# An attention layer split in two stages: q, k and v by seven block products in pairs of channel tiles, through DRAM, then the attention with its output projection

## The chip, the cores and the metric

The kernel runs on one core of a Trainium2 chip. The metric is the device time of one execution in microseconds (us), the median of several. The core has a matmul engine (TensorE, PE in the profile, its weight loads PEld), a vector engine (VectorE, DVE), a scalar engine (ScalarE, ACT), GpSimd (POOL), a sync engine that issues DMAs (SyncE, SP) and 16 DMA engines. TensorE writes into eight PSUM banks of 128 x 512 fp32 values.

## What is computed

The model has two layers on x of 1024 tokens by 1024 channels, all in fp32. Layer 0 mixes tokens by a gated and a convolved branch, layer 1 by attention; each is followed by a feed-forward block (FFN) with a short convolution. Only layer 1's attention is touched:

```python
h = rms_norm(x, odd_norm_g[j])
qkv = (h @ odd_w_qkv[j]).reshape(bn, s, 3, ATTN_HEADS, HEAD_DIM)
q = rotary(qkv[:, :, 0], pos)
k = rotary(qkv[:, :, 1], pos)
v = qkv[:, :, 2]
o = dilated_attention(q, k, v).astype(x.dtype).reshape(bn, s, D_MODEL)
x = x + o @ odd_w_o[j]
```

There are 16 heads of 64 channels. `dilated_attention` is the sum of three dilated patterns; the kernel computes it as one causal softmax over all keys with an additive mask that holds the logarithm of how many patterns see a key. The large products `h @ w_qkv`, `h @ w_up`, `act @ w_down` and `o @ w_o` take most of TensorE's time.

## The kernel before, in words

**Precision.** Every fp32 operand of a product is split into a high part, rounded on ACT (`hi_of`, L196), and the remainder, computed on DVE (`lo_of`, shown at L128). `mm3` (L256) then issues three matmuls for each 128 x 128 by 128 x 512 block: high x high, high x low, low x high.

**Order.** There is one program for all engines, written in order of ticks. `after(n, f)` puts work n ticks later, `tick()` moves on, and `tick` stands in the product loops about every six matmuls. So each engine has a fixed instruction order, and the DMAs have SP's. A product loop is a generator whose pieces are called units here.

**FFN up (`ffn_up`, L933).** Two pairs of channel tiles are computed plainly (`plain`), each with 96 matmuls. All further pairs are computed as a 2 x 2 block product with seven products in place of eight (`Pair`, L1094), each of 4 x 3 matmuls, 84 for a pair. The weights' sums are made on POOL (`plan`, L1020), the activations' sums once on DVE (`t_sums`), snapshots of running sums are copied by ACT (L1103).

**Attention (`attention`, L1301).** `prepare(hp)` (L1370) projects k, q and v of one pair of heads: 24 units, each of 6 matmuls into `psu` (`up_units`, L407). `rotate` (L1329) applies the rotary embedding on DVE (swap by four DMAs, two multiplications with `cos` and `sin`, one sum), then splits. `stack` copies halves of these into `k` and `st` tiles by DMAs within SBUF. `fin_v` turns v by eight transposes. All 24 units of the next pair of heads are spread over the 20 attention steps of this one by `feed`, 1.2 units a step. The loop over `steps` runs 8 head pairs x 2 heads x 10 steps. `scores` issues the score matmuls (L1430, L1431) `LEAD` = 4 steps early, `top` adds the mask and takes the maximum on DVE, `ex` takes the exponential on ACT (L1447). A step's `turn` (L1482) transposes probabilities into `ppt` and ACT and DVE split them into `tt`; `value` (L1505), two steps later, multiplies by v into `po`. ACT copies one half of `po` and DVE adds the other. `finish_pair` (L1532) scales by the inverse sums, turned and spread through DRAM, and stores `o`. The output projection runs in three groups of head pairs (`O_GROUPS`): the first within the last steps, the others behind them. `late` starts FFN 1's weights, and `then` starts FFN 1's norm for each finished token tile.

## Time and profile before

| | |
|---|---|
| median of 3 runs | 2233.28 us (2233.07 to 2234.79) |
| the profiled execution's own time | 2233.69 us |
| its span, first to last instruction | 2232.0 us |
| PE, DVE, ACT, POOL busy | 98%, 72%, 49%, 32% of the span |
| TensorE's granted clock | 0.994 of full speed |
| the attention, from its first projection to FFN 1's first product | 592.5 us |

Rows of a timeline say when an instruction started, how long it took and, in brackets, how long its engine sat idle before it and who released it. A window's row gives, for each engine, busy time and instructions within that stretch. Matmuls overlap: a single one shows some 0.39 us, but the next starts some 0.23 us after it, so time on TensorE is counted here from start to start. The attention's stretch has two parts: some 50 us of projections alone and then the steps, with projections laid between them.

### The profile page before, as it was taken

The numbers are of one execution on the slowest core, as the hardware profiler recorded it, in microseconds if no ns is written. First come the engines' busy times: TensorE is split into PE (matmuls) and PEld (weight loads), VectorE is DVE, ScalarE is ACT, GpSimd is POOL, SyncE is SP. The second block draws the span as 40 slices with busy tenths as digits, with TensorE's granted clock in tenths as the row PEclk, the third lists the DMA queues.
The fourth block names the chain that finished last, engine by engine and source line by source line (L and its number), as shares of the span: only waits on it lengthen the run. The fifth ranks groups of instructions, "written<-read, shape, count | busy, mean of one in ns | idle before, by whom it ended". The sixth has DMA issues, their size and how long they took to land.

```text
span 2232.0 us, 29238 instructions
## 1 busy us (share of the span) xinstructions
PE 2182.1 (98%) x10448; PEld 1823.9 (82%) x10448; DVE 1613.6 (72%) x2576; ACT 1098.1 (49%) x1667; POOL 705.8 (32%) x540
## 2 busy tenths in 40 slices
PE   6999899999999999999999999999999999999998
PEld 6888778888888888877888888788788888888886
DVE  6998668777777764565777777786787777777556
ACT  5345265444444545253555555654554444444532
POOL 1122033766666330040000000102456666653001
PEclk9999999999999999999999999999999999999999
DMA  5478422353534497446344444732134435349933
GB/s 185 108 140 182 148 95 73 126 184 132 193 128 175 174 363 278 142 170 152 89 107 118 123 106 123 202 110 97 66 132 154 172 136 185 132 151 346 368 133 115
DMA packets 138834, 352.13 MB, mean 158 GB/s; under 512 B 16448, under 2 KB 16832, under 8 KB 138688
## 3 DMA queue, kind: packets, MB, share of 16 engines
q1 hardware_dynamic: 133072, 329.90, 44.0%
q0 software_dynamic: 5616, 20.36, 4.6%
q8 instruction: 82, 1.34, 0.2%
q14 instruction: 64, 0.52, 0.1%
HBM read 216.01 MB, written 100.64 MB: 142 GB/s over the span
## 4 chain that ended last, share of the span: by engine, by line
PE 49%; DVE 2%; issue 2%; ACT 1%; DMA 1%; POOL 0%; DVEq 0%; POOLq 0%; ACTq 0%; SPq 0%
PE psd L1245 9%; PE psu L259 4%; PE psu L260 4%; PE psu L258 4%; PE po L1517 3%; PE psb L1069 3%; PE psb L1066 3%; PE psb L1067 3%; PE psc L1066 2%; PE psc L1069 2%; PE psc L1067 2%; PE ppt L1498 2%; PE pss L1430 2%; PE pss L1431 2%; PE ppt L1497 1%
## 5 line engine op out<-in xcount | busy, mean ns | idle before, releaser
L1245 PE MATMUL psd<-ab 128*128 128x512 f32 x1800 | 410.1, 389 | 0.0
L1245 PEld LDWEIGHTS psd<-ab 128*128 128x128 f32 x1800 | 337.7, 188 | 69.8
L258 PE MATMUL psu<-hTh,w 128*128 128x512 f32 (+1 forms) x592 | 237.0, 400 | 2.0 <-ACT hTh L196 2.0
L259 PE MATMUL psu<-hTl,w 128*128 128x512 f32 (+1 forms) x592 | 229.6, 388 | 0.2 <-DVE hTl L128 0.2
L260 PE MATMUL psu<-hTh,w 128*128 128x512 f32 (+1 forms) x592 | 229.5, 388 | 0.0
L196 ACT CAST ab<-ab 128x1024 fp32r<-128x1024 f32 x150 | 156.0, 1052 | 139.4 <-PE psd L1245 57.5
L128 DVE TENSOR_TENSOR ab<-ab,ab 128x1024 fp32r<-128x1024 f32 x150 | 189.8, 1320 | 33.3 <-ACT ab L196 32.8
L128 DVE TENSOR_TENSOR x<-psd,x 128x512 f32<-128x512 f32 x152 | 102.1, 687 | 140.3 <-PE psd L1245 112.6
L128 POOL MEMSET tt<- 128x256 f32 x64 | 20.0, 313 | 462.1 <-PE po L1517 261.7
L1103 ACT COPY sn<-psb 128x512 f32<-128x512 f32 x120 | 70.4, 587 | 170.7 <-PE psb L1069 128.0
L128 POOL TENSOR_TENSOR y<-y,y 128x512 f32<-128x512 f32 x66 | 95.1, 1441 | 182.2 <-DMA act<-y 115.7
L128 DVE TENSOR_TENSOR tt<-ppt,tt 128x512 fp32r<-128x512 f32 (+1 forms) x160 | 101.3, 634 | 46.5 <-ACT tt L196 45.4
L196 ACT CAST tt<-ppt 128x512 fp32r<-128x512 f32 (+1 forms) x160 | 86.7, 542 | 97.9 <-PE ppt L1498 88.2
L260 PEld LDWEIGHTS psu<-hTh,w 128*128 128x128 f32 x592 | 112.2, 189 | 23.3
L258 PEld LDWEIGHTS psu<-hTh,w 128*128 128x128 f32 x592 | 112.5, 190 | 19.1 <-ACT hTh L196 2.2
L259 PEld LDWEIGHTS psu<-hTl,w 128*128 128x128 f32 x592 | 112.7, 190 | 17.6 <-DVE hTl L128 0.5
L128 POOL TENSOR_TENSOR s<-wr 128x512 f32<-128x512 f32 x40 | 82.5, 2064 | 119.5 <-DVE psa L128 100.7
L128 DVE TENSOR_TENSOR wl<-wr,wh 128x1024 fp32r<-128x1024 f32 x88 | 119.7, 1361 | 0.0
L128 POOL TENSOR_TENSOR sm<-sm,mhalf 128x1 f32<-128x1 f32 (+2 forms) x38 | 31.3, 825 | 274.3 <-DVE sm L128 274.3
L1447 ACT ACTIVATE p<-p,sma 128x896 f32<-128x896 f32 (+7 forms) x128 | 99.5, 778 | 37.2 <-DVE sma L128 36.6
L1517 PE MATMUL po<-tt,v 128*128 128x256 f32 x640 | 108.3, 291 | 5.0 <-DVE tt L128 3.4
L128 DVE TENSOR_TENSOR pse<-psc,sn 128x512 f32<-128x512 f32 x40 | 28.0, 699 | 115.7 <-ACT sn L1103 115.7
(253 smaller groups left out, 5869.0 us busy)
## 6 DMA issues: line engine op xcount, KB each, us to landing
wr<-in_w_up_dram SPq DMA_DIRECT2D x88, 512.0 KB, 4.4
ab<-act SPq DMA_DIRECT2D x154, 256.0 KB, 5.4
act<-y SPq DMA_DIRECT2D x66, 512.0 KB, 2.9
wq<-in_w_down_dram SPq DMA_DIRECT2D x44, 512.0 KB, 5.3
wt<-wq SPq DMA_DIRECT2D x44, 512.0 KB, 4.5
ab<-wt SPq DMA_DIRECT2D x88, 256.0 KB, 5.4
ab<-in_w_down_dram SPq DMA_DIRECT2D x66, 256.0 KB, 5.6
wr<-in_w_qkv_dram SPq DMA_DIRECT2D x24, 512.0 KB, 3.9
```

What stands on the lines that cost most here:

```text
L128: return fn(*args, **kw)
L196: nc.scalar.copy(hi, src)
L258: nc.tensor.matmul(out_ap, st[0], mv[0], start=first, stop=False)
L259: nc.tensor.matmul(out_ap, st[0], mv[1], start=False, stop=False)
L260: nc.tensor.matmul(out_ap, st[1], mv[0], start=False, stop=last)
L1066: nc.tensor.matmul(ps, st[0], mv[0], start=f, stop=False, skip_group_check=True)
L1067: nc.tensor.matmul(ps, st[0], mv[1], start=False, stop=False, skip_group_check=True)
L1069: nc.tensor.matmul(ps, st[1], mv[0], start=False, stop=e, skip_group_check=True)
L1103: nc.scalar.copy(self.sn[key], self.b)
L1245: nc.tensor.matmul(ps, a[:, c], b[:, HALF:D], start=first and k == 0, stop=last and k == 2, skip_group_check=True)
L1447: nc.scalar.activation(p, p, AF.Exp, bias=sm[:, 2:3], scale=0.125, accum_out=lsum[hp][:, c:c + 1])
L1517: nc.tensor.matmul(po[:, c], v2[:, kb, :], tt[:, z, 256 * n:256 * n + 256], start=(g == 0 and n == 0 and z == 0), stop=(g == j and n == 1 ...
```

## The change

The attention becomes a class with two stages. `ffn_up`'s machinery is pulled out as `up_phase`, and FFN and attention both use it.

**First stage (`project`).** q, k and v are computed as 11 pairs of channel tiles by `up_phase`: v of heads 0 to 7 in two plain pairs, then nine pairs by seven block products (eight of a k and a q tile, one of two v tiles). A tile is copied out by ACT; k and q are rotated as before, v is turned as before, and the high and low parts are stored to DRAM (`store`): 48 DMAs of 512 KB in all, 32 of them for k and q. The norm ahead of it now also copies the transposed tiles (`raw`) and stores four of them (`keep`).

**Second stage (`run`).** The twelfth pair (v of heads 12 to 15) is computed plainly as the first filler (`late_units`), after its block of activations is fetched again. `load_set` fetches k, q and v of a head pair from DRAM in seven DMAs: six of 512 KB, each into 64 partitions, for k and q, and one of 1 MB for v; that of the next pair is issued ten ticks into a pair's 20 steps. Score matmuls keep their number and size but multiply the stacked high and low parts of k by q's high part and then by q's low part. The scaled minimum replaces the maximum and its scaling by a small DVE instruction. `LEAD` is 7, `VLAG` 4. The zero blocks of `tt` are set once, in four tiles. ACT copies both halves of `po`; their sum and the scaling by the inverse sums move from DVE to POOL (but for the last head pair). Scores of a head start at the steps that `S_STEPS` lists.

**Fillers.** `units` has 16 units of the late pair, 16 of the output projection for head pairs 0 and 1, and 32 for 2 to 4; `feed` asks for 0.25 to 0.4 units a step, and a filler that isn't ready gives its place up. Head pairs 5 to 7 are projected at the end, six banks opened ahead of the last head pair's part. x goes through DRAM between these groups.

**Queues.** The loads of mask, cos and sin move from POOL's queue to SP's, the store of the inverse sums from SP's to ACT's.

```diff
-O_GROUPS = ((0, 1, 2), (3, 4), (5, 6, 7))
+O_GROUPS = ((0, 1), (2, 3, 4), (5, 6, 7))
...
+QKV_ORDER = (("v", 0), ("v", 1), ("kq", 0), ("kq", 1), ("kq", 2), ("kq", 3),
+             ("kq", 4), ("kq", 5), ("kq", 6), ("kq", 7), ("v", 2), ("v", 3))
...
+LEAD = 7
+VLAG = 4
+SET_AT = 11
+O_PACE = 5
+O_LAST_AT = 12
+O_OPEN = 6
+S_STEPS = ((3, 0, 0), (3, 1, 1), (2, 0, 4), (2, 1, 5), (0, 0, 7), (0, 1, 8), (1, 0, 8), (1, 1, 9))
+LATE_SPLIT = 6
+LATE_FIRST = 6
+O_RATES = (0.25, 0.25, 0.3, 0.3, 0.3, 0.4, 0.4, 0.4)
...
+        def __init__(self, raw=False, keep=None):
...
+                if hT.keep is not None and i >= 4:
+                    nc.sync.dma_start(hT.keep[i - 4], src[0])
...
+    def up_phase(n_pairs, src, consumer, each=lambda j: None):
...
+            def src(j):
+                kind, n = QKV_ORDER[j]
+                ms = (KT + n, n) if kind == "kq" else (2 * KT + 2 * n, 2 * KT + 2 * n + 1)
+                return [io["w_qkv"][m].rearrange("p k c -> p (k c)") for m in ms]
...
+            def each(j):
+                if j == N_PLAIN:
+                    self.cos, self.sin = (stile(name=k) for k in ("cos", "sin"))
+                    nc.sync.dma_start(self.cos, io["cos"])
+                    nc.sync.dma_start(self.sin, io["sin"])
+                if j == len(QKV_ORDER) - 2:
+                    self.mask = stile(name="mask")
+                    nc.sync.dma_start(self.mask, io["mask"])
+                    after(SET_AT, lambda: self.load_set(0))
+                    after(2, self.late_weights)
+            self.start, self.products = up_phase(len(QKV_ORDER) - 1, src, self.heads, each)
...
+        def late_block(self):
+
+            raw = htile([P, 4, HALF], F32, "hr")
+            nc.sync.dma_start(raw, self.hT.keep.rearrange("i p c -> p i c"))
...
+        def late_units(self):
+            j = len(QKV_ORDER) - 1
+            outs, cv = {}, self.heads(j)
+            for t in range(2):
+                while t and not self.late_ready:
+                    yield "wait"
+                yield from up_units(self.hT, self.late_w, outs,
+                                    lambda n, t: cv.put(n, t, outs[(n, t)]), halves=(t,))
...
+            class Take:
+                def put(self, n, t, c):
+                    if not seen[n]:
+                        raw[n] = stile(name="r" + kind)
+                    nc.scalar.copy(raw[n][:, t * HALF:(t + 1) * HALF], c)
...
+                        if kind == "kq":
+                            att.rotate(raw[n], (att.q if n else att.k)[m])
+                        else:
+                            att.turn_v(raw[n], 2 * m + n)
+            return Take()
...
+            def store():
+                for z in range(2):
+                    nc.sync.dma_start(dst[z], f32v(st["hl"[z]]))
...
+        def load_set(self, hp):
...
+            def load(t, z, src):
+                nc.sync.dma_start(f32v(t[z * HD:(z + 1) * HD, :, :]),
+                                  src.rearrange("(e p) s -> p e s", e=2))
+
+            def first():
+                st["q1"], st["k"] = htile([P, 2, S], name="q"), htile([P, 2, S], name="k")
+                for z in range(2):
+                    load(st["q1"], z, self.q[hp, 0])
+                for z in range(2):
+                    load(st["k"], z, self.k[hp, z])
+
+            def second():
+                q2, v = htile([P, 2, S], name="q"), htile([P, 2, S], name="v")
+                for z in range(2):
+                    load(q2, z, self.q[hp, 1])
+                nc.sync.dma_start(f32v(v), self.v[hp].rearrange("e p s -> p e s"))
+                self.sets[hp] = (st["k"], (st["q1"], q2),
+                                 v.rearrange("p e (t c) -> p e t c", c=P))
+            first()
+            after(2, second)
...
+                    for z in range(2):
+                        nc.tensor.matmul(ps[:, :ws], qs[z], k[:, a:a + ws],
+                                         start=z == 0, stop=z == 1)
...
+                after(1, top, 1)
+                after(5, ex, 2)
...
+            def diag_tiles():
+                for _ in range(VLAG):
+                    tt = stile([P, 2, HALF], F32R, name="ttd")
+                    pool.memset(f32v(tt[:, :, 0:P]), 0.0)
...
+                after(1, lambda: hi_of(tt[:, 0, c:], pt[:, c:]))
+                after(3, lambda: lo_of(tt[:, 1, c:], pt[:, c:], tt[:, 0, c:]))
...
+                        outs_o[hp] = [stile(name="o") for _ in range(2)]
...
+                        for z in range(2):
+                            o = outs_o[hp][z][e * HD:(e + 1) * HD,
+                                              half * HALF:(half + 1) * HALF]
+                            nc.scalar.copy(o, po[z * HD:(z + 1) * HD, :])
...
-                    vec.tensor_tensor(o, po[HD:P, :], o, op=ALU.add)
...
+                eng = vec if hp == KT - 1 else pool
...
+                    eng.tensor_tensor(o, o, o2, op=ALU.add)
...
+                    nc.scalar.dma_start(l_dram[hp], st["row"])
...
+                def f():
+                    eng.tensor_tensor(o, o, st["r"], op=ALU.mult)
+                    if hp < KT - 1:
+                        nc.sync.dma_start(o_dram[hp], o)
+                        if hp == O_GROUPS[0][-1]:
+                            after(4, lambda: group(O_GROUPS[0]))
...
+                after(9, d)
+                after(15, f)
...
+            def group(ks):
+                for m, (k, w) in enumerate((k, w) for k in ks for w in (True, False)):
+                    after(1 + O_PACE * m, lambda k=k, w=w: fetch(k, w))
...
+            def units():
+                yield from self.late_units()
+                for n, ks in enumerate(O_GROUPS[:-1]):
+                    while ks[0] not in xgs or not ready(ks):
+                        yield "wait"
...
+                        if i + 2 < NT:
+                            x_load(xs, i + 2)
+                        yield from down_units([o_acts[k] for k in ks], [w_o[k] for k in ks],
+                                              xs, store, tiles=[i])
+                    if n < len(O_GROUPS) - 2:
+                        after(1, lambda n=n: group(O_GROUPS[n + 1]))
...
+                    elif got == "wait":
+                        state["want"] = state["done"]
+                        break
...
+            diag_tiles()
+            while self.tails:
+                self.tails.popleft()()
+            self.late_block()
+            for _ in range(LATE_FIRST):
+                feed(1)
+                tick()
+            for gi in range(-LEAD, 0):
+                for a in s_at.get(gi, ()):
+                    do_scores(*a)
+                feed(1)
+                tick(2)
+            for gi, step in enumerate(steps):
+                hp = step[0]
+                if gi == len(steps) - O_LAST_AT:
+                    group(O_GROUPS[-1][:-1])
+                if gi % 20 == 0:
+                    after(2 * VLAG + 2, lambda hp=hp: self.load_set(hp + 1))
+                for a in s_at.get(gi, ()):
+                    do_scores(*a)
+                feed(O_RATES[hp] / 2)
+                tick()
+                turn(*step)
+                feed(O_RATES[hp] / 2)
+                if gi >= VLAG:
+                    value(*steps[gi - VLAG])
+                tick()
...
+
+            for b in banks[:O_OPEN]:
+                part(b, range(n))
+            tk.until(lambda: ready(ks))
+            late()
+            f = then(xn)
...
+        hT = Normed(True, dpool.tile([4, P, HALF], F32, tag="keep", name="keep")
+                    if ph == "attn" else None)
 
...
+        up["attn"] = Attention()
+        up["attn"].start()
...
-    attention(x_drams["attn"], hT, nxt.then, lambda: ffn_start(1))
+    att, hT = up["attn"], nxt.hT
+    att.project(hT)
+    nxt = Next("ffn1")
+    att.run(x_drams["attn"], nxt.then, lambda: ffn_start(1))
```

## Rows read from the trace of the kernel before

**Rows 1.** The page, busy time of TensorE, its share of the span and instructions

```profile
PE 2182.1 (98%) x10448; PEld 1823.9 (82%) x10448; DVE 1613.6 (72%) x2576; ACT 1098.1 (49%) x1667; POOL 705.8 (32%) x540
```

**Rows 2.** The page, the chain that ended last, by engine

```profile
PE 49%; DVE 2%; issue 2%; ACT 1%; DMA 1%; POOL 0%; DVEq 0%; POOLq 0%; ACTq 0%; SPq 0%
```

**Rows 3.** Windows: stretch, length, engines' busy time, clock, DMA share, GB/s; attention

```profile
986.40:1578.90 592.50, 583.91 (x3273) 501.89 (x3274) 430.33 (x949) 324.47 (x640) 58.67 (x88) 0.99 0.45 124
```

**Rows 4.** Windows, one head pair's steps with the next pair's projections

```profile
1246.15:1306.50 60.35, 60.35 (x355) 52.42 (x354) 46.17 (x106) 35.14 (x72) 2.81 (x9) 1.00 0.44 114
```

**Rows 5.** Timeline of TensorE: start, length, operation; two runs of six projection matmuls

```profile
1242.96 0.39 PE L258 MATMUL psu<-hTh,w 128*128 128x512 f32 x1
...
1244.33 0.27 PE L1497 MATMUL ppt<-ident,p 128*128 128x128 f32 x1
...
1252.77 0.40 PE L258 MATMUL psu<-hTh,w 128*128 128x512 f32 x1
...
1254.17 0.27 PE L1497 MATMUL ppt<-ident,p 128*128 128x128 f32 x1
1254.28 0.27 PE L1498 MATMUL ppt<-ident,p 128*128 128x128 f32 x1
```

**Rows 6.** Waits of TensorE in the attention's stretch: total, times, longest

```profile
PE po L1517 <- DVE tt L128: 3.4, 2, 3.3
PE pss L1430 <- DMA st<-rl: 2.2, 1, 2.2
PE psu L258 <- ACT hTh L196: 2.0, 1, 2.0
```

**Rows 7.** Timeline of VectorE and of GpSimd around the longest wait

```profile
1438.44 1.22 DVE L128 TENSOR_TENSOR rl<-rq,rh 128x1024 fp32r<-128x1024 f32 x1
1439.57 3.38 DVE L128 TENSOR_TENSOR w<-wr,w 128x1024 fp32r<-128x1024 f32 x1
...
1439.41 8.12 POOL L128 TENSOR_TENSOR o<-ot,o 128x1024 fp32r<-128x1024 f32 x3 [8.16 <-ACT o L196]
```

**Rows 8.** Windows, six us just behind that wait

```profile
1443.00:1449.00 6.00, 5.53 (x26) 4.82 (x27) 4.29 (x12) 3.61 (x7) 4.77 (x3) 0.72 0.97 303
```

**Rows 9.** Windows, the two FFNs' first two pairs, plain, until the block products

```profile
341.50:387.80 46.30, 46.30 (x218) 38.53 (x218) 44.38 (x66) 23.52 (x38) 15.08 (x11) 1.00 0.18 57
1578.90:1630.60 51.70, 48.29 (x218) 39.71 (x217) 43.65 (x67) 27.93 (x44) 15.85 (x11) 0.97 0.17 62
```

**Rows 10.** TensorE's timeline, second product of two neighbouring block pairs, FFN 0

```profile
500.08 0.39 PE L1066 MATMUL psa<-hTh,wh 128*128 128x512 f32 x1
...
519.12 0.39 PE L1066 MATMUL psa<-hTh,wh 128*128 128x512 f32 x1
```

**Rows 11.** Windows, that block pair's 19.04 us

```profile
500.08:519.12 19.04, 19.04 (x85) 15.77 (x84) 14.89 (x22) 9.16 (x12) 12.50 (x8) 1.00 0.21 70
```

**Rows 12.** Groups of that pair on VectorE: busy, mean ns, idle before

```profile
L128 DVE TENSOR_TENSOR y<-y,y 128x1024 f32<-128x1024 f32 x2 | 2.4, 1220 | 0.0
...
L128 DVE SCALAR_TENSOR_TENSOR y<-psb,fcw,y 128x510 f32<-128x510 f32 x1 | 0.8, 750 | 0.0
```

**Rows 13.** Windows by tile, one head pair (PE, PEld, DVE, ACT): p, tt

```profile
1246.15:1306.50 60.35, 11.11 (x72) 8.86 (x72) 13.75 (x24) 13.81 (x32) 1.00 0.44 114
1246.15:1306.50 60.35, 13.42 (x81) 11.66 (x81) 12.70 (x20) 10.83 (x20) 2.81 (x9) 1.00 0.44 114
```

**Rows 14.** Timeline of ScalarE, back to back

```profile
1255.45 0.56 ACT L196 CAST tt<-ppt 128x512 fp32r<-128x512 f32 x1
1255.92 0.58 ACT L1529 COPY o<-po 64x512 f32<-64x512 f32 x1
```

**Rows 15.** Windows with DMAs dense: eight 64-partition stack copies, then FFN down

```profile
1231.50:1241.50 10.00, 10.00 (x62) 8.81 (x61) 6.68 (x18) 5.23 (x12) 0.32 (x1) 1.00 0.98 222
800.00:840.00 40.00, 40.00 (x178) 33.12 (x177) 30.07 (x25) 18.55 (x18) 15.93 (x8) 1.00 1.02 377
```

**Rows 16.** DMA issues of one kind: KB each, median us to landing

```profile
wr<-in_w_qkv_dram SPq DMA_DIRECT2D x24, 512.0 KB, 3.9
```

696 lines of the change are left out of this document (339 added, 357 removed).

## The prediction, on record before the change was run

> **What bounds the kernel now.** I read the page first: TensorE is busy 98% of the span [rows 1], and the chain of work that ended last lies on it for 49% with nothing else above 2% [rows 2]. So the next question is what TensorE does where the change is, and that is a matter of windows. From the attention's first projection to FFN 1's first product it takes 592.5 us, 583.9 of them busy [rows 3]; in the steady part it has no gap at all: one head pair takes 60.35 us and TensorE is busy for 60.35 [rows 4], while VectorE has 46.17 and ScalarE 35.14. The projections laid between the steps are a filler. Two runs of six of them take 1.37 and 1.40 us from start to start, so 0.231 us each, and a transpose takes 0.11 [rows 5]. All waits of TensorE in the stretch are eight, 10.5 us; the three longest are shown [rows 6]. The reader should see that the saving must come from TensorE's own work, and that what is lost can come only from engines that today have slack.
>
> The stretch as a sum: 1152 projection matmuls at 0.231 are 266.1. A head pair without its filler is 60.35 - 144 x 0.231 - 9 transposes x 0.11 = 26.1, eight are 208.8. The output projection is 384 matmuls at 0.227 (a block pair's pace, 19.04 / 84 [rows 10]), 87.2. 72 turns of v and of the sums are 7.9, 64 transposes of FFN 1's norm 7.0. Together 577.0; with 10.5 of waits, 5.0 are left, about what half clock costs: an idle of 3.3 us [rows 6] is followed by a granted clock of 0.72 over 6 us [rows 8], 1.7 us lost, and there are three such places.
>
> **The change part by part.** *The new ledger without waits.* The first two pairs with the rest of the norm are the same program as FFN's first two, which took 46.3 and 51.7 us, copies and sums of the activations included [rows 9]; I take 48, nearer the first, since four token tiles of this norm are ready early, as there. Nine block pairs at 19.04 us [rows 10] are 171.4. The late pair is 96 x 0.231 = 22.2. Eight head pairs 208.8, output projection 87.2, turns 7.9, and 40 x 0.11 = 4.4 for the norm transposes that fall ahead of FFN 1. Sum 549.9: 42.6 less than now. That is the room in which all new waits must fit.
>
> *VectorE and GpSimd in the block pairs.* FFN's pair keeps VectorE busy 14.89 us [rows 11]. Its convolution goes (eight taps at 0.75, four corners of some 0.2, one product at 1.22 [rows 12]: 8.1), two rotations come (eight operations of a row's 1.22: 9.8), so 16.6 of 19.04. What speaks against a fit is that VectorE's operation took 3.38 us instead of 1.22 beside a sum on GpSimd [rows 7]. Were each of the four half-size GpSimd sums of a pair to hold VectorE for its own length (8.12 / 3 / 2 = 1.35), a pair would need 22.0 and eight pairs lose 24. FFN's pair has these four sums too and TensorE doesn't wait in it [rows 10, 11], so I take 2 of 0 to 24. The Trainium skill, page "SBUF — State Buffer", section "SBUF: two separate sides", says that a VectorE operation with two SBUF inputs and a GpSimd operation exclude each other for a whole instruction; the long row agrees, and by that rule the loss would be the 24.
>
> *Handover between the stages.* The last block pair's tails and six late units lie between the issue of the first set and the first scores, about 17 us. The old handover waited 2.2 us for a DMA [rows 6]. I take 2 of 0 to 6.
>
> *Steps without filler.* 64 units are spread by hand: 13 run ahead of the steps, three in the first 12 steps. The first output group needs head pair 1 finished, stored, fetched and split: issued ticks put it at about step 69; it lasts to step 117, and the next group is ready at about 140. So some 80 of 160 steps have attention alone, at 26.1 / 20 = 1.305 us on TensorE. There ScalarE needs, per head pair, 13.81 for p, 10.83 for tt [rows 13] and eight copies of `po` at 0.58 [rows 14], 29.3, or 1.46 a step; but back to back an operation starts 0.09 before its predecessor ends [rows 14], 44 times, so 25.3 or 1.27. VectorE has 13.75 + 12.70 [rows 13], 1.32, or some 1.25 with the same overlap; its 64-row sums and small scalings are gone. The loss is 0 to 80 x 0.16 = 12.8; I take 3, as the overlap is what the row shows and the leads (7 steps for scores, 4 for values) absorb bursts.
>
> *The sets.* Seven times the next head pair's set is issued in step 5 and its first score stands in step 13. The six DMAs needed are 3.15 MB. Eight steps give 10.4 us without filler, 13.8 or 14.9 with 0.3 or 0.4 units of 1.39 us; with the fillers where I put them the seven covers are 12.9, 10.4, 10.4, 12.1, 13.8, 14.9 and 10.4. The rows give two speeds: 377 GB/s with whole tiles in FFN down, 222 with 64-partition copies while the DMAs were as busy [rows 15]. A load of 512 KB lands 3.9 us after issue [rows 16], 2.5 more than at 377 GB/s. So a set takes 10.9 or 16.7 us: TensorE waits 1.4 or 32.0 in sum. I take 300 GB/s, midway, as the source is DRAM and not another 64 partitions: 13.0 us, waits of 9.
>
> *Half clock.* Each idle of two us or more costs 1.7 [rows 8]: three of them, 5; none to six otherwise.
>
> *Tail and the rest.* Ahead of the last head pair's part lie 20 dense units and six opened banks, some 29 us, over its finish of 15 ticks; x's trips through DRAM have two tiles of lead. If that cover fails, one load's 3.9 us a group. I take 2 of 0 to 6, and 2 for short waits as now.
>
> *At no price*, being off TensorE's path: the store of the sums on ScalarE's queue (eight), mask, cos and sin behind one pair's fetches on SP's, GpSimd's memsets gone and its sums of `o` added. On SP's queue a store of `o` waits for GpSimd, and the fetches of fillers behind it have 12 ticks before they are split; were that cover gone, a filler comes a step late and its place is only moved to the dense end.
>
> Sum of the waits: 2 + 2 + 3 + 9 + 5 + 2 + 2 = 25. 42.6 - 25 = 17.6 gained. Against the profiled execution's own 2233.69 us (span 2232.0, 1.7 around; the median is 2233.28, 0.02% less) that is **2216 us**.
>
> **The rivals.** *All covers hold.* Sets at 377 GB/s, engines overlapped, no half clock: waits of 8, 2199. For it: FFN's block pairs run without a wait [rows 10, 11].
>
> *The sets come late* (the other side). At 222 GB/s the seven sets cost 32.0 and six idles 10.2 at half clock, 42 where I have 14: 2216 + 28 = 2244, slower. It decides from waits and half clock of 31 us together, which is a set of some 12.6 us plus landing, 250 GB/s. For it: the six DMAs fill 64 partitions each, as the copies did [rows 15]. Against it: those copies also read from 64 partitions. The Trainium skill, page "SBUF — State Buffer", section "Can I just issue two DMAs to hit both halves?", says that transfers to the two halves serialize and the section on the port swizzle gives 196 to 218 GB/s for 64 partitions; the row of 222 agrees, and by that rule this rival is the outcome.
>
> *ScalarE or VectorE paces the steps* without overlap: 12.8 instead of 3, 2226.
>
> *The block pairs don't save*: GpSimd's sums hold VectorE, 24 instead of 2, 2238: the change then moves work without shortening it.
>
> **How the numbers follow.** A measurement of this kernel can tell about 0.2%, 4.5 us, from no change. Chances: forecast 0.54 (its own range, 2206 to 2229, is faster in 0.48, same in 0.04, slower in 0.02), all covers 0.12 (faster), pacing 0.08 (faster 0.07, same 0.01), no saving 0.07 (0.01, 0.04, 0.02), sets late 0.19 (0.03, 0.03, 0.13). Faster 0.71, same 0.12, slower 0.17. The range leaves out the better half of the best case and the far end of the late sets: 2198 to 2245.
>
> **What would show it.** The projections' stage should show pairs of 19.04 us and last some 220 us; with 20.8 or more the fourth rival holds. In the steps without filler a head pair should take 26 to 28 us; 29 or more with ScalarE or VectorE full is the third. TensorE's waits should name `pss` behind DMAs of q and k, about 9 us in all; 30 would be the second, near zero the first. Wrong altogether would be a wait that none of these rows has, such as PSUM banks held through the longer lags.

## The result, and the profile after

| | median | ratio to the kernel before, with its 95% interval |
|---|---|---|
| kernel before | 2233.87 us | |
| changed kernel | 2243.59 us | 1.0044, 1.0031 to 1.0057 |
| forecast | 2216 us, 2198 to 2245 | |

The change makes the kernel slower by 0.44%. The time lies at the upper edge of the range, on the other side of the forecast.

On the page TensorE is now busy 97% of the span [rows 1], and the chain that ended last lies on it for 77%, with 4% on DMAs, where it was 1% [rows 2]:

```profile
PE 2166.4 (97%) x10340; PEld 1810.0 (81%) x10340; DVE 1635.1 (73%) x2483; ACT 1153.5 (51%) x1780; POOL 796.6 (36%) x535
...
PE 77%; DMA 4%; DVE 3%; ACT 3%; issue 1%; POOL 1%; SPq 0%; POOLq 0%; ACTq 0%; DVEq 0%
```

The attention, from its first projection to FFN 1's first product, takes 600.1 us where it took 592.5 [rows 3], and it starts 2.0 us later. These are the windows of its parts (columns as in rows 3): the two plain pairs, the nine block pairs, the handover to the first turned probabilities, the steps, and the end from the last product with v.

```profile
988.46:1040.50 52.04, 51.32 (x241) 42.19 (x241) 39.36 (x57) 26.22 (x52) 16.15 (x11) 0.95 0.37 130
1040.50:1214.64 174.14, 173.40 (x768) 142.56 (x767) 148.17 (x132) 86.01 (x126) 67.24 (x40) 1.00 0.67 211
1214.64:1246.82 32.18, 27.30 (x128) 22.09 (x126) 16.30 (x35) 13.45 (x28) 0.00 (x0) 0.95 0.75 250
1246.82:1524.73 277.91, 256.31 (x1770) 232.85 (x1768) 214.58 (x572) 224.72 (x500) 49.39 (x21) 0.98 0.78 215
1524.73:1588.54 63.81, 57.91 (x269) 46.50 (x268) 33.07 (x63) 25.88 (x41) 16.87 (x12) 0.99 0.63 232
```

Length less busy time of TensorE is its idle time: 0.7, 0.7, 4.9, 21.6 and 5.9 us, 33.8 together. To see all that is lost, half clock too, I count each instruction of TensorE at the pace at which its kind follows itself without a gap (0.227 us for 512 columns, 0.176 for 384, 0.120 for 256, 0.108 for a transpose) and call the sum the work of a stretch:

| part | length | work | beyond the work |
|---|---|---|---|
| two plain pairs | 52.0 | 48.8 | 3.2 |
| nine block pairs | 174.1 | 172.7 | 1.4 |
| handover | 32.2 | 24.7 | 7.5 |
| steps | 277.9 | 244.7 | 33.2 |
| end | 63.8 | 55.6 | 8.2 |
| together | 600.1 | 546.4 | 53.7 |

By the same count the kernel before has 570.9 of work and 21.6 beyond it. So the change saves its 24.5 us of work (9 x 12 matmuls at 0.227) and loses 32 in waits and half clock, 25 of them idle time (33.8 us where [rows 3] has 8.6). A block pair is what it was to be, 19.04 us and TensorE busy throughout; the head pairs without filler are as well; three of those with filler are not. The windows: a block pair, then head pairs 1 to 4 and 6 from their first turn to the next pair's (head pairs are counted from 0; pair 5, with 34.40 us, is like its work).

```profile
1096.70:1115.74 19.04, 19.04 (x86) 15.77 (x84) 17.98 (x16) 9.11 (x13) 7.93 (x4) 1.00 0.69 222
1277.40:1303.90 26.50, 26.50 (x203) 24.94 (x202) 23.59 (x68) 25.84 (x62) 4.81 (x2) 1.00 0.74 180
1303.90:1330.80 26.90, 26.78 (x203) 25.02 (x202) 23.95 (x70) 26.27 (x62) 4.79 (x2) 1.00 0.71 184
1330.80:1371.60 40.80, 33.90 (x228) 29.28 (x227) 30.20 (x80) 31.57 (x69) 9.54 (x4) 1.00 0.88 233
1371.60:1412.60 41.00, 37.17 (x240) 33.79 (x239) 28.61 (x77) 27.56 (x62) 4.74 (x2) 0.92 0.82 217
...
1447.00:1487.60 40.60, 31.80 (x212) 28.42 (x211) 29.02 (x77) 32.96 (x71) 11.92 (x5) 0.92 0.80 230
```

Pairs 3, 4 and 6 hold 24, 36 and 9 matmuls of fillers, so 26.1 plus these at 0.227 would be 31.6, 34.3 and 28.1 us: they lose 9.2, 6.7 and 12.5. The longest waits of TensorE in the steps (in all, times, longest), and the only one on a set's transfer:

```profile
PE po L1637 <- DVE sma L142: 10.6, 2, 6.7
...
PE pss L1542 <- DMA q<-q_dram: 1.5, 1, 1.5
```

Here `po` holds the products with v, `pss` the scores, `p` the probabilities, and `sma` is the small tile of minima that VectorE writes together with `p`. The wait of 6.7 us, followed back through the timelines of ScalarE, SP, GpSimd, VectorE and TensorE (start, length, engine, operation, and in brackets the idle time before it and its releaser):

```profile
1459.23 0.31 ACTq L1673 DMA_DIRECT2D l_dram<-lrow  x1
...
1466.60 1.10 SPq L1679 DMA_DIRECT2D r<-l_dram  x2
...
1474.06 2.34 POOL L142 TENSOR_TENSOR o<-o,r 128x1024 f32<-128x1024 f32 x1 [5.52 <-DMA r<-l_dram]
...
1476.43 0.69 DVE L142 CUSTOM_DVE_ANT_0 p<-pss,mask 128x512 f32<-128x512 f32 x1 [7.50 <-POOL o L142]
...
1477.19 0.58 PE L1637 MATMUL po<-tt,v 128*128 128x256 f32 x1 [6.74 <-DVE sma L142]
```

Read it from the top: the 8 KB of inverse sums are stored at 1459.2 but the load that needs them goes out only at 1466.6, in two parts, and the second lands at 1473.9; GpSimd scales; and VectorE's `p` starts as that scaling ends. `p` doesn't read `o` or `r`: what it waits for is the buffer that the scaling gives free. So VectorE stands 7.5 us with the split of `tt` behind it, and TensorE behind that. From the store's issue to the end of the scaling it takes 19.4, 17.1 and 17.2 us for pairs 2, 3 and 5 (while pairs 3, 4 and 6 run), 15.1 for pair 4 and 9 to 12 for the others, and only in the three long ones does VectorE wait, 4.3, 5.0 and 7.5 us:

```profile
DVE p L142 <- POOL o L142: 16.9, 3, 7.5
```

So the buffers cover 15.1, 12.0 and 9.7 us of this chain in pairs 3, 4 and 6. The cover differs from pair to pair.

Why the store is late stands in the list of transfers (KB each, median us to landing) of the steps; before, l_dram's landed in 2.4 us:

```profile
q<-q_dram SPq DMA_DIRECT2D x28, 512.0 KB, 12.4
...
v<-v_dram SPq DMA_DIRECT2D x7, 1024.0 KB, 17.3
...
l_dram<-lrow ACTq DMA_DIRECT2D x7, 8.0 KB, 7.3
```

A set was in flight. The set of head pair 3, and the work of its due step (SP's timeline, then TensorE's in step 5 of pair 2 and at pair 3's first score):

```profile
1297.82 1.28 SPq L1499 DMA_DIRECT2D q<-q_dram  x2
...
1311.23 0.27 PE L1617 MATMUL ppt<-ident,p 128*128 128x128 f32 x1
...
1321.57 0.63 PE L1542 MATMUL pss<-k,q 128*128 128x512 f32 x2
```

The set goes out 13.4 us ahead of the step in which the program has it, as SP waits for semaphores and not for ticks; the last part of q lands at 1315.9, 18 us after the first issue, and is needed at 1321.6. While it runs the DMA engines are full at this rate:

```profile
1305.00:1313.00 8.00, 8.00 (x62) 7.46 (x61) 7.71 (x24) 7.84 (x20) 1.36 (x1) 1.00 1.03 223
```

That is the rate of the 64-partition copies, 0.98 and 222 GB/s [rows 15].

### The profile page after: what moved, and what is told of

It is laid out like the page before. It is cut to its first block, busy times and chain, and to the rows that moved or that the text cites. A ratio compares the mean times of both kernels' runs of the same rounds, so it can differ in the third digit from the quotient of the medians.

```text
span 2241.7 us, 29095 instructions
## 1 busy us (share of the span) xinstructions
PE 2166.4 (97%) x10340; PEld 1810.0 (81%) x10340; DVE 1635.1 (73%) x2483; ACT 1153.5 (51%) x1780; POOL 796.6 (36%) x535
## 4 chain that ended last, share of the span: by engine, by line
PE 77%; DMA 4%; DVE 3%; ACT 3%; issue 1%; POOL 1%; SPq 0%; POOLq 0%; ACTq 0%; DVEq 0%
PE psd L1275 17%; PE psb L1044 8%; PE psb L1041 8%; PE psb L1042 8%; PE psc L1044 4%; PE psc L1041 4%; PE psc L1042 4%; PE po L1637 3%; PE pss L1542 2%; PE psu L273 2%; PE psu L274 2%; PE psu L272 2%; PE psa L1044 2%; PE psa L1041 2%; PE psa L1042 2%; PE psd L274 2%
## 5 line engine op out<-in xcount | busy, mean ns | idle before, releaser
L210 ACT CAST wh<-wr 128x1024 fp32r<-128x1024 f32 x112 | 117.5, 1049 | 6.6 <-DVE rl L142 4.7
L142 DVE SCALAR_TENSOR_TENSOR acc<-h,cw,acc 128x1007 f32<-128x1007 f32 (+22 forms) x77 | 96.8, 1261 | 1.5
L1542 PE MATMUL pss<-k,q 128*128 128x512 f32 (+2 forms) x384 | 89.5, 347 | 7.0 <-DVE sma L142 2.6
L272 PE MATMUL psu<-hTh,wh 128*128 128x512 f32 x224 | 91.5, 408 | 3.7 <-ACT hTh L210 3.7
L273 PE MATMUL psu<-hTl,wh 128*128 128x512 f32 x224 | 89.8, 401 | 1.8 <-DVE hTl L142 1.8
L1204 ACT ACTIVATE y<-y 128x1024 f32<-128x1024 f32 x44 | 46.7, 1062 | 84.7 <-DVE y L142 84.7
L274 PE MATMUL psu<-hTh,wl 128*128 128x512 f32 x224 | 89.3, 399 | 0.0
L142 POOL TENSOR_TENSOR wq<-wq 128x512 f32<-128x512 f32 x44 | 78.4, 1784 | 29.8 <-issue 14.6
L142 DVE CUSTOM_DVE_ANT_0 p<-pss,mask 128x512 f32<-128x512 f32 (+3 forms) x128 | 71.0, 564 | 24.2 <-POOL o L142 16.9
L142 DVE SCALAR_TENSOR_TENSOR y<-psb,fcw,y 128x511 f32<-128x511 f32 (+3 forms) x160 | 76.9, 483 | 12.2 <-ACT y L1170 6.8
## 6 DMA issues: line engine op xcount, KB each, us to landing
q<-q_dram SPq DMA_DIRECT2D x32, 512.0 KB, 11.7
```

The costliest lines, as they stand in the source:

```text
L142: return fn(*args, **kw)
L210: nc.scalar.copy(hi, src)
L272: nc.tensor.matmul(out_ap, st[0], mv[0], start=first, stop=False)
L273: nc.tensor.matmul(out_ap, st[0], mv[1], start=False, stop=False)
L274: nc.tensor.matmul(out_ap, st[1], mv[0], start=False, stop=last)
L1542: nc.tensor.matmul(ps[:, :ws], qs[z], k[:, a:a + ws], start=z == 0, stop=z == 1)
```

## Experiments: is it the sets, and by which way

Theory A: a set of 4.2 MB at 222 GB/s delays the small transfers of the head pair before, and VectorE stands for a buffer. Rival B: lags, buffers and ScalarE's pace, whatever the DMAs do. Ratios are to the kernel before, run beside each; "idle" is TensorE's in the steps, 21.6 us in the changed kernel.

**Two sets only.**

```diff
+            if hp >= 2:
+                self.sets[hp] = self.sets[hp - 2]
+                return
```

> Head pairs 2 to 7 fetch nothing and use the q, k and v of pairs 0 and 1 instead; the instructions of all engines stay as they are. Theory A (a set of 4.2 MB delays the 8 KB store and the broadcast load of the inverse sums that are issued behind it, GpSimd's scaling comes late, the buffers it holds are missing for VectorE's next probabilities, TensorE waits): the store lands in 2 to 3 us instead of 6.1, VectorE's 16.9 us of waiting for GpSimd go to under 3, TensorE's idle time in the steps falls from 21.5 us to under 8, the time by 18 to 28 us to 2216 to 2226. Theory B (the longer lags of 7 and 4 steps and the steps without filler are short of buffers and of ScalarE whatever the DMAs do): not under 2236.

2228.8 us, ratio 0.9981 (0.9971 to 0.9991). The steps as a window, and two rows of the lists:

```profile
1248.22:1509.91 261.69, 251.77 (x1770) 228.62 (x1769) 214.57 (x572) 224.13 (x500) 49.52 (x21) 1.00 0.41 132
...
l_dram<-lrow ACTq DMA_DIRECT2D x8, 8.0 KB, 1.3
...
DVE p L142 <- POOL o L142: 2.0, 1, 2.0
```

Idle 9.9, and 16.2 us less in the steps: that is the price of the sets, half of all that the steps lose beyond their work. It lies in head pairs 3, 4 and 6 alone: here they take 37.4, 34.4 and 34.5 us, 16.1 less together, and the other five are within 0.3 us of what they were. Theory A holds, 3 us below the gain that it named, and B (not under 2236) is not the whole. The 9.9 us still idle have no set behind them; that B's lags, buffers and ScalarE's pace cause them is not shown. Without six of the sets the change is 0.2% faster than the kernel before, where its 24.5 us of saved work alone would be 1.1%.

**The q and k part earlier.** `third` loads v, 22 ticks after q and k.

```diff
+SET_STEP = 14
...
+            if late:
+                after(late, third)
...
-                if gi % 20 == 0:
-                    after(2 * VLAG + 2, lambda hp=hp: self.load_set(hp + 1))
+                if gi == 0:
+                    after(2 * VLAG + 2, lambda: self.load_set(1))
+                if gi % 20 == SET_STEP:
+                    self.load_set(hp + 2, 2 * (20 - SET_STEP) + 2 * VLAG + 2)
```

> The q and k part of a set is issued 11 steps earlier, in step 14 of the pair before the last, and v's 1 MB stays where it is, so that the store and the load of the inverse sums find 1 MB ahead of them and not 4.2 MB. Theory A: VectorE's waits for GpSimd under 5 us, the waits of 3.8 and 6.7 us at the value products gone, 12 to 20 us faster than the changed kernel, 2224 to 2232. Theory A2 (it is the volume in each pair, not the order, that delays the small transfers): within 4 us of 2243.6. Theory B: within 4 us as well.

2250.1 us, 1.0072 (1.0057 to 1.0087): slower. VectorE's and ScalarE's waits in the steps:

```profile
DVE p L143 <- POOL o L143: 2.0, 1, 2.0
...
ACT o L211 <- DMA ot<-o_dram: 10.2, 1, 10.2
ACT w L211 <- DMA wr<-in_w_o_dram: 8.8, 2, 5.7
```

The first row is what A forecast, and the gain is gone all the same: now ScalarE's splits wait in order for the fillers' transfers, which share the time with the sets. So the order chooses who waits. That the volume in a pair, at this rate, is what delays (A2) fits; but A2's time, within 4 us of 2243.6, was missed as well, by 2.5 us.

**The sum and the scaling of o back on VectorE.**

```diff
-                eng = vec if hp == KT - 1 else pool
+                eng = vec
```

> The sum of the two halves of o and the scaling by the inverse sums go back from GpSimd to VectorE for all head pairs. Theory A (the load of the inverse sums is late, and what waits for it holds up those behind): VectorE itself now waits for the load with the next probabilities behind it, so the waits grow: 4 to 25 us slower than the changed kernel. Rival E (GpSimd's 2.4 us in place of 1.2 is what makes the chain late): 3 to 8 us faster.

2251.9 us, 1.0075 (1.0059 to 1.0092), 7 to 8 us slower than the changed kernel; VectorE waits for the load itself, 26.3 us where it waited 16.9 for GpSimd:

```profile
DVE o L142 <- DMA r<-l_dram: 26.3, 6, 8.0
```

So GpSimd's slower scaling isn't the cause; it shelters VectorE from part of the lateness.

**A shorter lead.**

```diff
-LEAD = 7
+LEAD = 5
```

> The scores run 5 steps ahead in place of 7, so that a set is needed two steps (2.6 us) later and two steps' probabilities less are held. Theory A (VectorE's probabilities wait for a buffer that the scaling of o frees): VectorE's waits for GpSimd fall from 16.9 us to under 10, 3 to 8 us faster, as long as the shorter lead covers mask, exponential and turn. Theory B' (the lead is what lets ScalarE and VectorE absorb their bursts): the steps without filler go from 26.5 to over 28 us a head pair, 4 to 12 us slower.

2241.3 us, 1.0033 (1.0022 to 1.0045), some 2 us faster, which isn't clear of noise and less than A's 3 to 8. VectorE's wait for GpSimd:

```profile
DVE p L142 <- POOL o L142: 4.4, 1, 4.4
```

It is 4.4 us in place of 16.9, though the chain of the inverse sums still takes 17 to 19 us in four head pairs: with two steps' probabilities less to hold, the buffers cover more of it, so the link is the buffer. Head pairs without filler take 27.1. But idle is still 20.3 us: TensorE's turns now wait for the probabilities themselves, some 12 us, so what the buffers gave, the shorter lead took.

**The first set after the last swaps.**

```diff
-SET_AT = 11
+SET_AT = 15
```

> The first set is issued four ticks later, behind the four swap transfers of the last rotation. Theory A says that ScalarE's wait of 10.2 us for that rotation and TensorE's of 3.8 us behind it came from these swaps standing behind the set: they go to under 4 and under 0.5, and the time falls by 3 to 6 us to 2238 to 2241. The rival is that the first scores then wait for the set themselves, by the 4 to 5 us that it comes later: no gain, or up to 4 us lost.

2244.2 us, 1.0049 (1.0034 to 1.0064): no gain. ScalarE's wait for the last rotation fell from 10.2 to 2.4 us and TensorE's of 3.8 behind it went, as A said; but then the block of activations of the late pair (`hr`, 1 MB) stood behind the set, ScalarE waited 9.3 us for it and TensorE, behind ScalarE and VectorE, 6.0:

```profile
ACT hTh L210 <- DMA hr<-keep: 9.3, 1, 9.3
```

## Experiments: why a set is slow

Theory C: because each q or k transfer fills 64 partitions. A packet here is a row of 4 KB; share x 16 engines x 4096 bytes / rate is the time of one: 1.03 x 16 x 4096 / 223 GB/s = 303 ns. v's transfers fill 128. The Trainium skill, page "SBUF — State Buffer", section "Door 1: The DMA port swizzle", gives some 218 GB/s as the limit for 64 partitions and twice that for 128; 223 agrees with it.

**Both halves in one transfer.**

```diff
-                nc.sync.dma_start(f32v(t[z * HD:(z + 1) * HD, :, :]),
-                                  src.rearrange("(e p) s -> p e s", e=2))
...
+                    nc.sync.dma_start(f32v(t[:, e, :]), src(e))
...
+                return lambda e: x[e * HD:(e + 1) * HD, :].unsqueeze(0).to_broadcast([2, HD, S])
```

The source of a transfer is 2 x 64 rows of 1024.

> The same 3.15 MB of k and q of each set are fetched by six transfers into all 128 partitions (one for each half of the columns) in place of six into 64. Theory C (the set is slow because each transfer fills 64 partitions: 4 KB packets take 305 to 315 ns in them and 159 ns in v's, which fills 128): the packets take about 160 ns, a q or k transfer lands some 6 us after issue in place of 11.7, the waits behind the sets (16.2 us by the kernel with two sets) mostly go, time 2228 to 2234, and the first set's wait shrinks too. Rival D (the rate is that of reading DRAM while other transfers run): packets stay near 300 ns, time within 3 us of 2243.6.

2614.5 us, 1.1703 (1.1686 to 1.1721), which neither side forecast. A window in a set:

```profile
1385.00:1405.00 20.00, 3.03 (x18) 2.10 (x16) 3.40 (x12) 4.24 (x13) 0.00 (x0) 0.67 0.13 52
```

A share of 0.13 is two of 16 engines. The Trainium skill, page "DMA: Bandwidth & Descriptors", section "Rules for kernel authors", says that an outermost dimension smaller than 16 confines a transfer to as many engines; with two it agrees. The run tells nothing of C but that 0.13 x 16 x 4096 / 52 = 164 ns a packet.

**Two queues.**

```diff
-                nc.sync.dma_start(f32v(t[z * HD:(z + 1) * HD, :, :]),
+                (nc.scalar if z else nc.sync).dma_start(f32v(t[z * HD:(z + 1) * HD, :, :]),
```

> Of each pair of transfers that fill the two halves of a tile of q or k, the second is issued on ScalarE's queue, so that both halves are written at the same time. Theory C (a transfer into 64 partitions is slow because of where it writes): with both halves in flight the packets of 305 to 315 ns come down towards 160, the set takes some 11 us in place of 17, the fourth, fifth and seventh head pairs get shorter by 10 to 15 us in all, 2229 to 2235. Rival D (the rate is the same however the halves are ordered): packets stay at some 310 ns, and ScalarE's issues, 0.6 us each, cost another 0 to 4 us: 2243 to 2248.

2258.4 us, 1.0104 (1.0089 to 1.0119), 10 us beyond the slower forecast. It doesn't tell C from D: the halves were not written at once, as ScalarE reached its issue 7.7 us after SP:

```profile
1308.04 0.60 SPq L1499 DMA_DIRECT2D q<-q_dram  x1
...
1315.77 0.60 ACTq L1499 DMA_DIRECT2D q<-q_dram  x1
```

**q and k laid out in DRAM as in the tiles.**

```diff
+                    for e in range(2):
+                        x = f32v(st["hl"[z]])[e * HD:(e + 1) * HD, :]
+                        for d in range(2) if is_q else (z,):
+                            to = dst[z, e] if is_q else dst[e]
+                            nc.sync.dma_start(to[d * HD:(d + 1) * HD, :], x)
...
+                    nc.sync.dma_start(f32v(t[:, e, :]), src[e])
```

> q and k are laid out in DRAM as they stand in the tiles, q twice, so that each of the six transfers of a set fills 128 partitions from 128 rows of 4 KB; the stores ahead are cut into pieces of 64 rows and there are 1 MB more of them per block pair. The kernel with a two-part outer dimension kept only three DMA engines busy, at 159 ns a packet, so it did not tell theories C and D apart; this one does. Theory C: packets of some 160 ns on all engines, the set lands in 11 us, the waits of the steps fall from 33.2 us beyond the work to some 18 to 22, the block pairs keep 19.04 us: 2229 to 2234. Rival D: packets near 300 ns, no gain in the steps; and if the stores load the queue of the block pairs, some us more: 2243 to 2250.

2260.8 us, 1.0115 (1.01 to 1.013): both outcomes at once, in different stages. Block pairs, steps, and two transfers in the steps:

```profile
1043.17:1248.40 205.23, 184.54 (x768) 147.90 (x766) 149.32 (x132) 84.99 (x126) 64.92 (x40) 0.95 0.75 219
1283.94:1546.38 262.44, 253.35 (x1770) 230.03 (x1769) 214.01 (x571) 223.51 (x500) 49.50 (x21) 0.99 0.63 227
...
q<-q_dram SPq DMA_DIRECT2D x28, 512.0 KB, 7.2
...
l_dram<-lrow ACTq DMA_DIRECT2D x7, 8.0 KB, 2.1
```

The steps give back 15.5 us with the full volume still fetched, so C holds there. The block pairs lose 31; their stores are now twelve to a pair, in pieces of 64 rows, and 1 MB more, and this run alone doesn't part the two.

**Heads interleaved.** The channels of two heads stand alternately, and a tile of a set is every second of 256 rows: one stride, 128 partitions, whole stores.

```diff
-                    nc.sync.dma_start(dst[z], f32v(st["hl"[z]]))
+                    for to in (dst[z, 0], dst[z, 1]) if is_q else (dst[z],):
+                        nc.sync.dma_start(to, f32v(st["hl"[z]]))
...
+                rows = src.rearrange("z (p e) s -> e (z p) s", e=2)
+                    nc.sync.dma_start(f32v(t[:, e, :]), rows[e])
...
+        "w_qkv": heads_mixed(up(i["odd_w_qkv"][0])),
```

> The channels of the two heads of a q or k tile stand alternately (the columns of the weights and the rows of cos and sin are permuted for it), so that a tile of a set is every second row of 256 rows in DRAM: each of the six transfers fills 128 partitions with one stride, k needs no other store than before, q is stored twice in whole tiles (1 MB more a block pair), and a rotation's swap takes two transfers in place of four. Theory C: packets of 160 ns in the sets, the steps lose about 16 us less as with the relaid sets, and the block pairs keep 19.04 us as their stores are whole: 2226 to 2231 us, faster than the changed kernel by 13 to 17 and than the kernel before by 2 to 8. If the block pairs lose as with the relaid sets, it was the added volume and not the pieces: 2245 to 2260.

2231.6 us, 0.9991 (0.9982 to 1.0), 12 us faster than the changed kernel and 0.6 us past the far end of what was expected; the interval just reaches 1, so it is hardly clear of the kernel before. Block pairs, steps, a window in a set, and a store:

```profile
1041.25:1221.73 180.48, 174.99 (x768) 142.11 (x767) 145.98 (x132) 84.86 (x126) 68.50 (x40) 1.00 0.73 249
1252.26:1512.93 260.67, 251.55 (x1770) 228.74 (x1769) 213.72 (x571) 223.55 (x500) 49.50 (x21) 1.00 0.66 229
...
1310.00:1312.00 2.00, 2.00 (x17) 1.86 (x16) 2.00 (x9) 1.94 (x4) 0.00 (x0) 1.00 1.03 422
...
l_dram<-lrow ACTq DMA_DIRECT2D x8, 8.0 KB, 2.4
```

422 GB/s at the same share, 160 ns a packet, and the steps are as short as with two sets (260.7 to 261.7), though all sets are fetched. C is shown: the form of the transfers, not their bytes, cost the 16 us. The block pairs lose 6.3 with the same bytes stored as in the relaid sets, so some 25 of the 31 us there came with the pieces.

**The same with q stored once**, its four transfers back at 64 partitions, only k's two at 128 (the diff is that of the last, less its second store).

> Interleaved heads, but q is stored once, as in the changed kernel, and still fetched by four transfers into 64 partitions; only k's two transfers fill 128. A set then needs some 2.1 MB at 220 GB/s and 2.1 MB at 400, 15 us in place of 17 to 19. If the six us that the interleaved heads lose in the block pairs come from q's second store, they are back: 174 us from the first to the last block product. If the waits behind the sets have a threshold at the cover that the chain of the inverse sums has, most of the 17 us stay won (steps 18 to 24 us beyond their work): 2225 to 2231. If they go with the time of the set, a fifth of them: 2238 to 2241.

2234.7 us, 1.0007 (0.9995 to 1.0018), between the two forecasts. Block pairs, steps, VectorE's wait for GpSimd:

```profile
1041.08:1215.21 174.13, 173.35 (x768) 142.56 (x766) 150.16 (x132) 85.20 (x126) 67.78 (x40) 1.00 0.65 213
1247.13:1518.30 271.17, 254.71 (x1769) 232.53 (x1768) 214.01 (x571) 223.97 (x500) 49.51 (x21) 0.97 0.77 220
...
DVE p L142 <- POOL o L142: 10.9, 2, 10.2
```

The second store is what the block pairs paid for. TensorE has one long wait in the steps in place of three, of 9.1 us in pair 6; from the store of the sums to the end of the scaling it took 19.9 us there, 15.0 and 12.8 in pairs 3 and 4, and VectorE waited 10.2, nothing and 0.7. The chain less the wait gives 9.7 us in pair 6 and 12.1 in pair 4, the covers of the changed kernel again; in pair 6 it is 9.7 with two sets only and with interleaved heads too (a chain of 11.7, a wait of 2.0). So the loss has a threshold, but not one: what counts is by how much the chain exceeds the cover of its pair. The steps lost 26.5 us beyond their work, more than the 18 to 24 of the threshold's forecast, as a single chain was long where the cover is shortest.

## Experiments: the rest

**The last weight.** Two runs, the split 5 ticks after the fetch in place of 12, and the rows fetched 12 steps earlier and split where they were fetched, with the load of the norm's gain (in `then`) ahead of FFN 1's first weights:

```diff
-                after(12, parts)
+                after(n, parts)
...
-                        after(1, lambda: fetch(KT - 1, True))
+                        after(1, lambda: fetch(KT - 1, True, 5))
---
+                    after(2 + 4 * O_PACE, last_load)
...
-                        after(1, lambda: fetch(KT - 1, True))
+                        after(1, last_split)
...
+            f = then(xn)
             late()
-            f = then(xn)
```

> The weight rows of the last head pair are split 5 ticks after their fetch instead of 12. If the late weight (its split ended at 1552.8 us, with six banks open) is why the next norm starts late and TensorE waits for it in the last 30 us, the norm starts some 5 us earlier, these waits fall from about 6 to 2 us and the time by 3 to 5 us. If the norm's own chain over ScalarE, GpSimd and VectorE sets the pace there, the time stays within 1.5 us of 2243.6.

> The last head pair's weight rows are fetched some 12 steps earlier and split where they were fetched, and the norm's gain is issued ahead of FFN 1's first weights. Theory F (in the end SP's queue stands behind the stores of x, so that the last weight was issued at 1545 us, and the next norm starts late): the weight is split by about 1536 us, x's first tile is ready some 10 us earlier, the tail from the last product with v to FFN 1's first product falls from 63.8 to about 57 us, the time by 5 to 7 us to 2236.5 to 2238.5. Rival G (the norm's own pace of 5.5 us a tile over four engines is the limit): under 2 us gained.

2243.2 us, 1.0047 (1.0031 to 1.0064), and 2240.4, 1.003 (1.0018 to 1.0042). In the second the weight was split at 1545 us in place of 1553, yet x's first tile came only 2 us earlier, as the opened banks stand ahead of it; the end shortened from 63.8 to 63.0, FFN 1's first pairs by 2.4. The 3 us gained lie between F's 5 to 7 and G's 2, and the run doesn't part the weight from the gain's load. TensorE's waits in the end for the norm's `xn` are 3.6 us with and without the change, so the norm's own chain (G) stays where it was.

**The splits apart**, alone:

```diff
-O_PACE = 5
+O_PACE = 9
-                after(3 if hp < KT - 1 else 1,
+                after(6 if hp < KT - 1 else 1,
```

> The fetches of a group of the output projection stand 9 ticks apart in place of 5, and o counts as split after 6 ticks in place of 3. In the kernel with two sets the fourth and the seventh head pair still took 5.8 and 6.4 us more than their work. Theory H (four to six splits in a burst, 1.05 us each on ScalarE and 1.2 to 2.4 on VectorE or GpSimd, fall on steps in which these engines have no slack): these two head pairs get 3 us shorter each, the time falls by 3 to 7 us. Rival: the splits only come later, and fillers with them, to the dense end: within 2 us of 2243.6.

2249.1 us, 1.0068 (1.0053 to 1.0083): slower by 5.5, for a reason that neither side named: the fetches moved into the next set, and ScalarE waited for `ot`, a tile of `o` fetched again:

```profile
ACT o L210 <- DMA ot<-o_dram: 8.6, 2, 8.4
```

**Combinations:** relaid sets with the last weight; interleaved heads with the last weight; these with the splits 8 ticks apart; the same with q stored once; and with the second store 11 ticks later.

> The relaid sets together with the early last weight. The two losses lie in different stages, so the gains add: with theory C 2225 to 2232, 2 to 4 us under the relaid sets alone, which would be level with the kernel before or up to 8 us under it.

> Interleaved heads together with the early last weight, which alone gained 3 us: 2223 to 2229, some 3 us under the interleaved heads alone.

> As the last, with the fetches of a group 8 ticks apart in place of 5 and o counted as split after 6 ticks in place of 3. With slow sets this cost 5.5 us, as ScalarE stood waiting for o's transfers. Theory H (bursts of splits cost the fourth and the seventh head pair 5.8 and 6.4 us, and with fast sets nothing hides it any more): 3 to 6 us faster than with 5 ticks. Rival (fillers come later and are missing in the steps): 0 to 5 us slower.

> As the last, with the early last weight and the fetches of a group 8 ticks apart. With a threshold: 2222 to 2228, faster than both kernels. Without: ScalarE waits for o's transfers again as with the splits apart alone, 2240 to 2248.

> As the interleaved heads with the early last weight and the splits apart (2229.6), but q's second store is issued 11 ticks later, behind the next block pair's swaps, which it delayed (a swap landed 3.7 us after issue in place of 2.3, with VectorE, ScalarE and TensorE behind it). If this delay is what the block pairs lost (180.5 to 181.8 us in place of 174.1), most of the 6 to 7 us come back: 2222 to 2226. If it is the buffers that q's parts hold until their second store, they are held longer now: 2230 to 2240.

| run | median | ratio | interval |
|---|---|---|---|
| relaid, last weight | 2258.3 | 1.0100 | 1.0083 to 1.0116 |
| interleaved, last weight | 2230.6 | 0.9990 | 0.9981 to 0.9999 |
| and splits apart | 2229.6 | 0.9983 | 0.9974 to 0.9993 |
| and q stored once | 2239.4 | 1.0032 | 1.0020 to 1.0043 |
| and second store later | 2230.2 | 0.9987 | 0.9978 to 0.9996 |

Only the last of these forecasts was met, by its second side (2230 to 2240). The relaid sets lost in the block pairs again; the early last weight gave 1 us beside interleaved heads, not 3.

The third row beats both kernels, the one before by 0.17%. The splits apart cost 5.5 us beside the sets of the changed kernel. Beside interleaved heads they gain about 1, which isn't clear of noise: pairs 3 and 6 take 33.4 and 31.6 us in place of 37.5 and 34.5, but they hold 12 and 9 filler matmuls less, and the dense end grows by 6 us, the work moved there (27 matmuls at 0.227). Beyond their work the two pairs lose 4.6 and 5.5 us in place of 6.0 and 6.4, so theory H has 2 of its 3 to 6 us. With q's slow transfers the splits apart lose again, to within 1 us of the forecast without a threshold; but that side's cause, ScalarE waiting for `ot`, isn't there: TensorE waits 5.9 us for GpSimd's split of `o` and 3.2 for q. Whether such a setting is good hangs on the sets. The second store later left the block pairs at 181.0 us, so it isn't their order; whether it is its bytes or the buffers that it holds stays open.

## Why the prediction was wrong, point by point

*The ledger.* Right: 549.9 us against 546.4 of work. Of its room of 42.6, however, only 24.5 is work; the rest was the old kernel's waits and half clock, taken as gone. (Of the 10.5 us of waits read there [rows 6] 2.0 lie ahead of the stretch's first product; idle in the stretch are 8.6 [rows 3].)

*Block pairs.* Right: 19.04 us, VectorE busy 17.98 of it where the working had 16.6. The rival by which VectorE and GpSimd shut each other out gave 24 us, and TensorE idles 0.7 us in these pairs. The rule beside it, of the Trainium skill, page "SBUF — State Buffer", section "SBUF: two separate sides", names a lock held for a whole instruction; if it is at work here, the slack of the stage hides it.

*Steps without filler.* Right: 26.5 and 26.9 us, of 26 to 28, with ScalarE busy 25.84 and 26.27. The pacing rival is out.

*The sets, the step whose mechanism failed.* The sum let a set go out in step 5 and priced only the first score's wait, at 300 GB/s. All three were wrong. The seven sets go out 4.5 to 18 us earlier than step 5, since the queue of SP isn't held to ticks; they run at 223 GB/s, the lower of the two rows that stood there [rows 15]; and the first scores wait 1.5 us for them, not 9. The cost lay on whoever else had a transfer then. The working had the store of the sums on ScalarE's queue "at no price", as off TensorE's path; but it takes 7.3 us to land in place of 2.4, and the buffers that its chain holds are the ones that VectorE needs. That is 16 us, half clock included, where 9 stood. VectorE's wait for a buffer that GpSimd frees is in none of the rows, the prediction's own sign of being wrong altogether.

*The rival of late sets* named 2244, and the time is 2243.6, but not by its mechanism: its root, 222 GB/s, was right, and the 32 us of waiting for q and k that it priced were 1.5. The long cover that it left out would have refuted it; the small transfers that it left out, and the terms below, made up for that. The agreement is luck.

*Handover, end, short waits.* 2, 2 and 2 us were taken; idle were 4.9 and 5.9, and the steps without sets still idled 9.9. The handover's cover of 17 us was filled by transfers that stand behind the first set, whichever (the swaps, or `hr`). At the end one weight waits on SP behind x's stores, and TensorE waits 3.6 us for the norm's chain. What keeps the steps without sets from their work, 17 us of which head pairs 3 and 6 have 12, is not shown; bursts of splits account for 2 at most by the splits apart. These terms were named and under-sized.

*First pairs.* 48 us were taken, nearer to FFN 0's 46.3 than to FFN 1's 51.7 [rows 9]; 52.0 it was, and the start came 2.0 later, TensorE waiting 3.7 us, where it waited 2.0, for the first `hTh` behind ScalarE's copies for `raw`. The second row was the nearer one.

*Half clock.* 5 us were taken; the granted clock of 0.95, 0.95, 0.98 and 0.99 over the windows above comes to about 10. Waits of 20 us were forecast and 33.8 are idle, and the two long ones in the steps cost more than 1.7 each: pairs 4 and 6 ran at 0.92 for 41 us, some 3.3 us lost in each.

In sum 53.7 us beyond the work stand against 28.5 in the forecast (25, and the 3.5 that its ledger lay above the work): 25 us, and 2 at the start, are the miss. By part, half clock counted where it fell: the steps apart from the sets 12.0 above what stood for them (17.0 against 3 and 2), the sets 7.2, the end 6.2, the handover 5.5, the first pairs 4.0 and their start 2.0, the block pairs 0.7; against them stand 10.5 that the forecast held without a place (5 of half clock, and 5.5 that its ledger lay above the work of the second stage). So the sets were mispriced in kind but are a quarter of the miss. They decide the sign (with two sets the change is 0.2% faster, with all 0.4% slower), yet even with two sets the kernel is 13 us above the forecast.

## What to carry to other kernels

Price a bulk load by what else must move while it runs, not by its own due time alone: a few KB that a chain of small steps stores and loads again is what stands behind it, and the buffers which that chain holds carry the delay to engines that share no data with it. The DMAs on SP's queue started here when their semaphores allowed, so take such times from the release of their buffers and not from the place in the program's schedule. And count the partitions that each transfer fills: a layout in DRAM that lets one stride fill all 128 was worth as much in these steps as not fetching at all, though its second store cost 6 us in the stage ahead.

## What the hardware showed that I had not expected

Reads from DRAM into 64 partitions ran at 223 GB/s with the DMA engines full, no better than the copies from 64 partitions within SBUF [rows 15], and at 422 as soon as each filled 128. A transfer of 512 KB whose outer dimension is two kept two engines busy, 52 GB/s, and made the kernel 17% slower. An 8 KB store on another queue took 7.3 us to land (the median of the steps) beside sets at 223 GB/s, 2.4 beside sets at 422 and 1.3 with two sets only.
